# Order of the products in a projection, and the loading of the first panel, in a two-layer decoder trunk

## The chip, the cores and the metric

The kernel runs on one core of a Trainium2 chip. The metric is device time in microseconds (us) for one execution, as the median of several. Profiles come from a separate profiled execution, whose own time is given beside its span (from its first to its last instruction).

## The reference, cut to what matters

A trunk of two layers over 256 tokens of width 2048, with 256 memory tokens:

```python
mem_n = rmsnorm(mem, norm_mem)
for i in range(2):
    if i == 1:
        fk, fv, fc = fox_shared_kv(x, fox_kv_norm, fox_w_kv, fox_b_f)
    mk, mv = memory_kv(mem_n, mem_w_kv[i])
    h = rmsnorm(x, norm_mix[i])
    # layer 0: gated linear attention, layer 1: forgetting attention, both with 4 memory heads
    x = x + (gla_mixer if i == 0 else fox_mixer)(h, ..., mk, mv, ...)
    h = rmsnorm(x, norm_ffn[i])
    x = x + conv_ffn(h, ffn_w_up[i], ffn_conv_w[i], ffn_conv_b[i], ffn_w_down[i])
return rmsnorm(x, norm_final)
```

Nearly all of the arithmetic is projections: an activation of 256 tokens times a weight matrix of 2048 (or 5632) rows. All inputs and weights are 32-bit floats.

## The kernel before, in words

**Products in parts.** TensorE takes the weights and activations in a 32-bit format of its own (`F32R`) that keeps fewer bits than a float. So each float is split into a high part (a copy rounded to `F32R`) and a low part (the float minus its high part). A product is then three products: high times high, high times low, low times high. Activations lie as `[128, 2, 256]` tiles (`bufA`, `bufB`), high part and low part side by side, so one 512-wide matmul multiplies a weight's high part by both parts of an activation ("wide" or "high" product), and one 256-wide matmul multiplies a weight's low part by the activation's high part ("narrow" or "low" product).

**Units.** Weights are packed in HBM (`wp`) in units of 128 partitions x up to 1024 columns (512 KB), in the order of their use. `split_unit` (L204) and `load_unit` (L187) handle one unit: SyncE (SP) issues a DMA into `raw` (4 buffers, L198), ScalarE (ACT) casts it into `whi` (3 buffers, L201), VectorE (DVE) subtracts to give `wlo` (3 buffers, L210). They are put 300 places ahead in the priorities (`AHEAD`) from which the framework's scheduler writes each engine's queue; each engine then works its queue in order.

**Two kinds of panel.** `proj_fm` (L213) makes 256 output features by 256 tokens from four units of four 128-row chunks each: weights stationary, activations moving, two PSUM accumulators (`c` = 0, 1). For a unit it runs 8 wide products (L233) and 8 narrow ones (L231); the last unit runs its narrow ones first. Since the last unit of a panel ends with wide ones and the next panel begins with wide ones, a panel is, on TensorE, 16 wide (8 of them the last panel's), 8 narrow, 8 wide, 8 narrow, 8 wide, 16 narrow. `proj_tm` (L246) has the tokens stationary and up to 512 weight columns moving; it isn't changed but for the number of `wlo` buffers.

**What follows a panel.** An `evac` function takes the accumulator apart: `whole` (ACT L241, DVE L243), then, for an up-projection (`ffn`, 88 of the panels), a scaling (L860), the causal convolution (ACT L864, DVE L865, L866), the gate (L869, L870) and the split of the result (L306, L307). These share ACT's and DVE's queues with the casts and subtractions of the next units.

**The start.** `WARM` = 12 matmuls on a cleared tile (L178) come first. The first panel, `("mk", 0, 0)`, multiplies the memory. `take_mem` (L454) loads the memory in four groups of four chunks (`memt`; the gains of its norm lie ahead of the first group) and splits each chunk (`split`, L302: ACT L309 scales to the high part, DVE L310 computes the low part), beside the loads of the four units of weights, which are cast and subtracted in two pieces each. The first group's first half is issued on ACT's DMA queue, everything else on SP's. After the panel the squares of the memory are summed for its norm (L492 to L501).

**The end.** The last projection's `last` (L931) handles two blocks `b` of 128 tokens: it adds the accumulator to the residual `x[3]`, squares it, multiplies it by the final gain into `y` (L942), gets the root of the mean (L944 to L953), multiplies the four 512-wide parts by it (L957, L959) and stores each (L960), part 1 through ACT's queue and the others through SP's.

**Others that the change touches.** `att` (L529), two `[128, 384]` tiles cleared by GpSimd (POOL, L534), holds the attention of a linear-attention head. `mk[0]` holds the memory keys of layer 0; `mem_parts` (L412) splits it into parts and nothing reads it afterwards.

Of the kernel before, what the change touches and what calls it, by code (L numbers as in the profile page):

```python
# [12 lines left out]
F32 = mybir.dt.float32  # L13
# [28 lines left out]
WARM = 12  # L42
# [96 lines left out]
def _trunk(ctx: ExitStack, tc: tile.TileContext, xt, xtok, memt, wp, wgu, gns, gfin, cnv, par, msk, out):  # L139
# [30 lines left out]
    mk = [const.tile([P, MEM_H, T], F32, name=f"mk{l}") for l in range(2)]  # L170
# [16 lines left out]
    def load_unit(unit, pieces=1, before=None, pool=wpool, whole=False):  # L187
        off, kcs, n = unit
        w = len(kcs) * n
        raw = wpool.tile([P, NUNIT], F32, name="raw", tag="raw", bufs=4)  # L190
        hi = pool.tile([P, NUNIT], F32R, name="whi", tag="whi", bufs=3)
        src = wp[off : off + P * w].rearrange("(p n) -> p n", p=P)
        for i in range(pieces):
            if before is not None:
                before(i)
            s = slice(i * w // pieces, (i + 1) * w // pieces)
            if not whole:
                loads.append(nc.sync.dma_start(raw[:, s], src[:, s]))  # L198
            elif i == 0:
                loads.append(nc.sync.dma_start(raw[:, :w], src))  # L200
            casts.append(S.activation(hi[:, s], raw[:, s], AF.Copy))  # L201
        return raw, hi, w

    def split_unit(unit, pieces=1, before=None, pool=wpool, whole=False):  # L204
        with tc.high_priority(offset=AHEAD):
            raw, hi, w = load_unit(unit, pieces, before, pool, whole)
            lo = pool.tile([P, NUNIT], F32R, name="wlo", tag="wlo", bufs=3)
            for i in range(pieces):
                s = slice(i * w // pieces, (i + 1) * w // pieces)
                V.tensor_tensor(lo[:, s], raw[:, s], hi[:, s].bitcast(F32), ALU.subtract)  # L210
        return hi, lo

    def proj_fm(key, src, evac, before=None):  # L213
# [6 lines left out]
        for n, unit in enumerate(units):  # L220
            if before is None:
                hi, lo = split_unit(unit)
            else:
                hi, lo = split_unit(unit, 2, lambda half: before(n, half), whole=n > 0)
            steps = [(c, j, src[kc - base]) for j, kc in enumerate(unit[1]) for c in range(2)]
            final = n == len(units) - 1
            for part in ((1, 0) if final else (0, 1)):
                for c, j, both in steps:
                    s = slice(j * 256 + c * P, j * 256 + (c + 1) * P)
                    if part:  # L230
                        TE.matmul(acc[c][:, :T], lo[:, s], both[:, 0, :], start=False, stop=False)  # L231
                    else:
                        TE.matmul(acc[c], hi[:, s], both, start=n == 0 and j == 0,  # L233
                                  stop=final and j == len(unit[1]) - 1)
# [67 lines left out]
    def split(dst, i, src, g=None):  # L302

        hi, lo = dst[i][:, 0, :], dst[i][:, 1, :]
        if g is None:
            S.activation(hi, src, AF.Copy)  # L306
            V.tensor_tensor(lo, src, hi.bitcast(F32), ALU.subtract)  # L307
        else:
            S.activation(hi, src, AF.Copy, scale=g)  # L309
            V.scalar_tensor_tensor(lo, src, g, hi.bitcast(F32), ALU.mult, ALU.subtract)  # L310

# [138 lines left out]
    with tc.tile_pool(name="load", bufs=1) as lp:  # L450
        mraw = [lp.tile([P, KC + 4 * T], F32, name=f"mt{i}") for i in range(4)]
        mt = [t[:, KC:].rearrange("p (c t) -> p c t", t=T) for t in mraw]

        def take_mem(g, half):  # L454

# [577 lines left out]
```

## Time and profile before

| | |
|---|---|
| median of 3 runs | 2286.44 us (2286.3 to 2286.55) |
| the profiled execution | 2286.35 us |
| its span | 2284.6 us |
| TensorE matmul, busy | 2273.0 us, 12420 matmuls |
| VectorE, busy | 1613.1 us |
| ScalarE, busy | 1245.6 us |
| GpSimd, busy | 3.2 us, 20 instructions |
| read from HBM | 425.87 MB |

How to read it: PE is TensorE's matmuls and PEld its weight loads, DVE is VectorE, ACT ScalarE, POOL GpSimd, SP SyncE; a `q` behind the name is the engine's sequencer, which waits and issues DMAs. L210 is line 210 of the kernel before. In a group, `out<-in` are the tiles, then the count, busy us and mean ns of one, and after a second bar the idle time of the engine ahead of the group with what ended it. Matmuls overlap and their ends are modelled, so the time of a matmul is read from one start to the next. In the timeline a row is start us, length us, engine, line and what it does, merged over neighbours of one kind.

### The profile page before, as it was taken

Reading aid. Unit: us, or ns where it says so; the run is one execution under the profiler, and the core shown is the slowest. Engines: PE = TensorE matmul, PEld = TensorE weight load, DVE = VectorE, ACT = ScalarE, POOL = GpSimd, SP = SyncE. Lnnn points to the kernel's source line nnn. Section 1 sums busy time; section 2 is a strip of 40 time slices with the busy share of each in tenths; the row PEclk is TensorE's granted clock in tenths of the full one; section 3 lists DMA queues with packets and bytes.
Section 4 is the critical chain, followed back from the end, with each engine's and each line's share of the span. In section 5 each row is a group of like instructions: output and inputs, shape, how many; then the busy total and the mean of one; then the engine's idle time right before and its main releaser. Section 6 shows DMA issues by size and latency. Waiting matters only on the chain.

```text
span 2284.6 us, 33316 instructions
## 1 busy us (share of the span) xinstructions
PE 2273.0 (99%) x12420; PEld 1983.1 (87%) x12420; DVE 1613.1 (71%) x2691; ACT 1245.6 (55%) x1981; POOL 3.2 (0%) x20
## 2 busy tenths in 40 slices
PE   9999999999999999999999999999999999999998
PEld 8889988888888888888888998888888888888886
DVE  8679997577765777567766568657776577756775
ACT  7556555555543555445565555556554455534554
POOL 0000000000000000000000000000000000000000
PEclk9999999999999999999999999999999999999999
DMA  9555555555555555555555664556555655555564
GB/s 330 190 166 162 164 164 189 184 187 192 185 194 194 189 189 187 195 190 190 190 184 186 181 196 158 178 186 186 192 186 192 193 188 191 189 195 188 189 191 155
DMA packets 124746, 430.16 MB, mean 188 GB/s; under 512 B 14108, under 2 KB 18600, under 8 KB 124456
## 3 DMA queue, kind: packets, MB, share of 16 engines
q1 hardware_dynamic: 124152, 427.24, 57.7%
q8 instruction: 97, 1.59, 0.3%
q10 hardware_dynamic: 432, 0.79, 0.1%
q14 instruction: 65, 0.53, 0.1%
HBM read 425.87 MB, written 2.11 MB: 187 GB/s over the span
## 4 chain that ended last, share of the span: by engine, by line
PE 99%; DVE 1%; DMA 0%; issue 0%; ACT 0%; DVEq 0%
PE acc L233 39%; PE acc L271 36%; PE acc L231 20%; PE ps_s L890 0%; PE ps_s L645 0%; PE ps_t L402 0%; PE ps_s L423 0%; PE ps_o L423 0%; DVE A L310 0%; PE ps_s L802 0%; PE ps_o L818 0%; PE ps_o L689 0%; DVE wlo L210 0%; DMA raw<-wp 0%; PE ps_s L801 0%; PE ps_o L690 0%
## 5 line engine op out<-in xcount | busy, mean ns | idle before, releaser
L210 DVE TENSOR_TENSOR wlo<-raw,whi 128x1024 fp32r<-128x1024 f32 (+4 forms) x812 | 971.3, 1197 | 446.5 <-ACT whi L201 431.4
L201 ACT ACTIVATE whi<-raw 128x1024 fp32r<-128x1024 f32 (+4 forms) x812 | 842.1, 1038 | 634.7 <-PE acc L271 327.0
L233 PE MATMUL acc<-B,whi 128*128 128x512 f32 x2112 | 524.0, 392 | 0.0
L233 PEld LDWEIGHTS acc<-B,whi 128*128 128x128 f32 x2112 | 382.1, 189 | 69.9
L271 PE MATMUL acc<-whi,mix 128*128 128x512 f32 x1280 | 320.3, 390 | 0.0
L233 PE MATMUL acc<-mix,whi 128*128 128x512 f32 x1248 | 315.7, 393 | 0.0
L231 PEld LDWEIGHTS acc<-B,wlo 128*128 128x128 f32 x2112 | 280.7, 191 | 15.8 <-DVE wlo L210 0.2
L231 PE MATMUL acc<-B,wlo 128*128 128x256 f32 x2112 | 288.2, 283 | 0.0
L271 PEld LDWEIGHTS acc<-whi,mix 128*128 128x128 f32 x1280 | 239.7, 188 | 49.8
L233 PEld LDWEIGHTS acc<-mix,whi 128*128 128x128 f32 x1248 | 227.1, 188 | 42.0
L241 ACT ACTIVATE part<-acc 128x256 f32<-128x256 f32 x240 | 90.2, 376 | 243.8 <-PE acc L233 243.6
L271 PE MATMUL acc<-whi,B 128*128 128x512 f32 (+3 forms) x960 | 217.9, 362 | 0.0
L243 DVE TENSOR_TENSOR wholes<-acc,part 128x256 f32<-128x256 f32 x240 | 100.8, 420 | 133.5 <-ACT part L241 133.5
L271 PEld LDWEIGHTS acc<-whi,B 128*128 128x128 f32 x960 | 174.5, 188 | 17.7
L231 PEld LDWEIGHTS acc<-mix,wlo 128*128 128x128 f32 x1248 | 171.4, 190 | 12.2
L231 PE MATMUL acc<-mix,wlo 128*128 128x256 f32 x1248 | 177.0, 283 | 0.0
L271 PE MATMUL acc<-wlo,mix 128*128 128x512 f32 x640 | 173.9, 390 | 0.0
L271 PEld LDWEIGHTS acc<-wlo,mix 128*128 128x128 f32 x640 | 119.9, 188 | 24.8
L233 PE MATMUL acc<-A,whi 128*128 128x512 f32 x544 | 136.5, 393 | 0.3 <-DVE A L310 0.2
L864 ACT ACTIVATE cv<-u,cw 128x256 f32<-128x256 f32 x176 | 105.0, 598 | 46.5 <-DVE u L860 46.5
L271 PE MATMUL acc<-wlo,B 128*128 128x512 f32 (+3 forms) x480 | 120.8, 363 | 0.9 <-DVE wlo L210 0.9
L233 PEld LDWEIGHTS acc<-A,whi 128*128 128x128 f32 x544 | 97.8, 189 | 18.7 <-DVE A L310 0.7
(225 smaller groups left out, 1602.0 us busy)
## 6 DMA issues: line engine op xcount, KB each, us to landing
raw<-wp SPq DMA_DIRECT2D x743, 512.0 KB, 3.5
raw<-wp SPq DMA_DIRECT2D x32, 384.0 KB, 3.3
raw<-wp SPq DMA_DIRECT2D x24, 388.0 KB, 3.6
raw<-wp SPq DMA_DIRECT2D x8, 400.0 KB, 3.2
xf<-xt SPq DMA_DIRECT2D x16, 128.0 KB, 4.8
x<-xtok SPq DMA_DIRECT2D x4, 512.0 KB, 8.4
mt<-memt SPq DMA_DIRECT2D x3, 512.0 KB, 6.5
cb<-cdram SPq DMA_DIRECT2D x12, 128.0 KB, 3.3
```

The lines of the kernel that those rows point to most:

```text
L201: casts.append(S.activation(hi[:, s], raw[:, s], AF.Copy))
L210: V.tensor_tensor(lo[:, s], raw[:, s], hi[:, s].bitcast(F32), ALU.subtract)
L231: TE.matmul(acc[c][:, :T], lo[:, s], both[:, 0, :], start=False, stop=False)
L233: TE.matmul(acc[c], hi[:, s], both, start=n == 0 and j == 0, stop=final and j == len(unit[1]) - 1)
L241: S.activation(t, a[:, T:], AF.Copy)
L243: V.tensor_tensor(r, a[:, :T], t, ALU.add)
L271: mm = TE.matmul(acc[b][:, :n], src[kc - base][:, part, xs], w, start=u == 0 and low == part == j == 0, stop=u == end and low == 1 and j = ...
L864: S.activation(r, u[:, 2:], AF.Identity, bias=w[3], scale=w[2])
```

## The change

The core of the diff (lines that only rename or pass an argument are left out):

```diff
-WARM = 12
+WARM = 9
...
+    def split_unit(unit, pool=wpool):
...
+            raw = wpool.tile([P, NUNIT], F32, name="raw", tag="raw", bufs=4)
+            hi = pool.tile([P, NUNIT], F32R, name="whi", tag="whi", bufs=3)
+            lo = pool.tile([P, NUNIT], F32R, name="wlo", tag="wlo", bufs=4)
...
+        if before is None:
+            turns = [(0, 0), (1, 0), (0, 1), (1, 1), (2, 1), (3, 1), (2, 0), (3, 0)]
+        else:
+            turns = [(0, 0), (0, 1), (1, 0), (1, 1), (2, 0), (2, 1), (3, 1), (3, 0)]
+        ready = {}
+        chunks = [(u, low, j) for u, low in turns for j in range(4)]
+        if before is not None:
+            chunks[:8] = sorted(chunks[:8], key=lambda t: t[2])
+        for u, low, j in chunks:
+            if u not in ready:
+                ready[u] = split_unit(units[u]) if before is None else before(u, units[u])
+                if u == 1 and between is not None:
+                    between()
+            w, both = ready[u][low], src[units[u][1][j] - base]
+            for c in range(2):
+                s = slice(j * 256 + c * P, j * 256 + (c + 1) * P)
+                if low:
+                    TE.matmul(acc[c][:, :T], w[:, s], both[:, 0, :], start=False, stop=False)
+                else:
+                    TE.matmul(acc[c], w[:, s], both, start=u == j == 0, stop=(u, j) == (3, 3))
...
     def split(dst, i, src, g=None, alone=False):
...
-            S.activation(hi, src, AF.Copy, scale=g)
+            done = V.tensor_scalar(hi, src, g, None, ALU.mult) if alone else S.activation(hi, src, AF.Copy, scale=g)
             V.scalar_tensor_tensor(lo, src, g, hi.bitcast(F32), ALU.mult, ALU.subtract)
...
+        lead = [lp.tile([P, KC + 4 * 512], F32, name=f"ld{g}") for g in range(2)]
+        pair = [t[:, KC:].rearrange("p (c k t) -> p c k t", k=2, t=T) for t in lead]
+        mt = [t[:, :, 1, :] for t in pair]
+        mt += [lp.tile([P, 4, T], F32, name=f"mt{g}") for g in range(2, 4)]
+
+        def first_unit(g, unit):
+            off, kcs, n = unit
+            hi = wpool.tile([P, NUNIT], F32R, name="whi", tag="whi", bufs=3)
+            lo = wpool.tile([P, NUNIT], F32R, name="wlo", tag="wlo", bufs=4)
             if g == 0:
+                S.preload_act_table_set("natural_log_exp_and_others")
+            with tc.high_priority(offset=AHEAD):
+                if g < 2:
+                    step = 1 if g == 0 else 2
+                    for c in range(0, 4, step):
+                        at = slice(KC + c * 512 if c else 0, KC + (c + step) * 512)
+                        if g:
+                            at = slice(KC + c * 512, KC + (c + step) * 512)
+                        loads.append(nc.sync.dma_start(lead[g][:, at], memt[g, :, at]))
+                    w = pair[g][:, :, 0, :]
+                else:
+                    step = 2
+                    raw = wpool.tile([P, NUNIT], F32, name="raw", tag="raw", bufs=4)
+                    loads.append(nc.sync.dma_start(raw, wp[off : off + P * NUNIT].rearrange("(p n) -> p n", p=P)))
+                    loads.append(nc.sync.dma_start(mt[g].rearrange("p c t -> p (c t)"), memt[g, :, KC : KC + 4 * T]))
+                    if g == 2:
                         nc.sync.dma_start(gains, gns)
+                    w = raw.rearrange("p (c t) -> p c t", t=T)
+                for c in range(0, 4, step):
+
+                    for i in range(c, c + step):
+                        k = 4 * g + i
+                        done = split(bufA, k, mt[g][:, i, :], lead[0][:, k : k + 1], i % 2 == 1)
+                        if i % 2 == 0:
+                            casts.append(done)
+                    cs = slice(c, c + step)
+                    h3, l3 = (t.rearrange("p (c t) -> p c t", t=T)[:, cs, :] for t in (hi, lo))
+                    casts.append(S.activation(h3, w[:, cs, :], AF.Copy))
+                    nc.gpsimd.tensor_tensor(l3, w[:, cs, :], h3.bitcast(F32), ALU.subtract)
+            return hi, lo
...
+        proj_fm(("mk", 0, 0), bufA, first_out, before=first_unit)
+        proj_fm(("mk", 0, 1), bufA, mk_out(0, 1), between=squares)
...
-            for t in (*att, *ks):
+            for t in ks:
                 nc.gpsimd.memset(t, 0.0)
...
             kv = mem_parts(0, "A")
+
+            lent = const.tile([P, MEM_H, T], F32, name="att", tag="mk0").rearrange("p f t -> p (f t)")
+            nc.gpsimd.memset(lent, 0.0)
+            att = [lent[:, i * 3 * P : (i + 1) * 3 * P] for i in range(2)]
...
-            V.tensor_tensor(y[:, b, :], x[3][:, b, :], gf[:, 3 * 512 :], ALU.mult)
...
-            for g in range(4):
-                t = y[:, b, :] if g == 3 else x[g][:, b, :]
-                if g == 1:
+            for f, lo, hi in ((0, 0, T), (1, 0, 512), (0, T, 512), (2, 0, 512), (3, 0, 512)):
+                t = x[f][:, b, lo:hi]
+                if f == 1:
                     S.activation(t, t, AF.Copy, scale=r)
+                elif f < 3:
+                    V.tensor_scalar(t, t, r, None, ALU.mult)
                 else:
-                    V.tensor_scalar(t, t, r, None, ALU.mult)
-                (nc.scalar if g == 1 else nc.sync).dma_start(out[b, :, g * 512 : (g + 1) * 512], t)
+                    V.scalar_tensor_tensor(t, t, r, gf[:, 3 * 512 :], ALU.mult, ALU.mult)
+                (nc.scalar if f == 1 else nc.sync).dma_start(out[b, :, f * 512 + lo : f * 512 + hi], t)
```

What it does, part by part:

- **Order of the products.** In every panel of `proj_fm` but the first, the units' products run as high 0, high 1, low 0, low 1, low 2, low 3, high 2, high 3. Each unit is loaded, cast and subtracted whole; `wlo` has four buffers.
- **The first panel.** The first two groups of memory and the first two units of weights lie interleaved in one array, 256 columns of weights beside 256 columns of memory. Group 0 is loaded in four pieces, group 1 in two, groups 2 and 3 as weights and memory apart, all on SP's queue. The first unit's products alternate by chunk, two wide and two narrow. Every second memory chunk's high part is computed on DVE, the others on ACT; the weights are cast on ACT and their low parts subtracted on POOL, in pieces of 256 columns (unit 0) or 512 (the others).
- **The squares** of the memory come inside the second panel, behind its second unit's load.
- **The warm-up** has nine matmuls.
- **`att`** lies in the place of `mk[0]`, and is cleared once `mem_parts` is through.
- **The end.** `y` is gone: part 3 is multiplied by the root and the gain in one instruction. Part 0 is scaled and stored in two halves, around part 1.

More of the change, by code (lines that the diff above doesn't have):

```diff
@@ L219, in proj_fm @@
         base = min(min(u[1]) for u in units)
[L220 to L234, printed above, removed]
+        if before is None:
[18 more added lines that the diff above has]
+                    TE.matmul(acc[c], w[:, s], both, start=u == j == 0, stop=(u, j) == (3, 3))
         for c in range(2):
```

81 lines of the change are left out of this document (26 added, 55 removed).

## The prediction

> **What bounds the kernel now.** I read first the totals and the chain that ended last on the page, then the groups of the three projection lines, then the timeline of one up-projection, of the first 20 us and of the last 10 us.
>
> ```profile
> PE 2273.0 (99%) x12420; PEld 1983.1 (87%) x12420; DVE 1613.1 (71%) x2691; ACT 1245.6 (55%) x1981; POOL 3.2 (0%) x20
> ...
> PE 99%; DVE 1%; DMA 0%; issue 0%; ACT 0%; DVEq 0%
> ...
> L233 PE MATMUL acc<-B,whi 128*128 128x512 f32 x2112 | 524.0, 392 | 0.0
> L233 PE MATMUL acc<-mix,whi 128*128 128x512 f32 x1248 | 315.7, 393 | 0.0
> L233 PE MATMUL acc<-A,whi 128*128 128x512 f32 x544 | 136.5, 393 | 0.3 <-DVE A L310 0.2
> ```
>
> PE is busy for 99% of the span and is 99% of the chain. L233, the 512-wide high product of `proj_fm`, has 2112 + 1248 + 544 = 3904 matmuls. A panel has 32 of them, so there are 122 such panels, each with 32 narrow low products (L231) beside them. PE waits for nobody there: idle before it is 0.0 or 0.3 us. What can still go is what PE spends inside its own stream, what it waits for in the first panel, and the end after its last product.
>
> One panel, on PE alone (start, length, line, tiles, count; the next row's start tells when a run is over, the printed lengths overlap):
>
> ```profile
> 599.78 1.48 PE L231 MATMUL acc<-B,wlo 128*128 128x256 f32 x11
> 601.10 3.82 PE L233 MATMUL acc<-B,whi 128*128 128x512 f32 x16
> 604.76 1.12 PE L231 MATMUL acc<-B,wlo 128*128 128x256 f32 x8
> 605.71 2.00 PE L233 MATMUL acc<-B,whi 128*128 128x512 f32 x8
> 607.55 1.11 PE L231 MATMUL acc<-B,wlo 128*128 128x256 f32 x8
> 608.50 2.00 PE L233 MATMUL acc<-B,whi 128*128 128x512 f32 x8
> 610.34 2.08 PE L231 MATMUL acc<-B,wlo 128*128 128x256 f32 x16
> ```
>
> And rows of the chain in order of time (start, length, count):
>
> ```profile
> 844.45 3.65 PE acc L233 x16
> 877.91 3.65 PE acc L233 x16
> 913.21 87.04 PE acc L271 x384
> ```
>
> A 512-wide product in a long run takes 87.04 / 384 = 0.2267 us. A 256-wide one inside a run takes (601.10 - 599.78) / 11 = 0.120 us. A panel therefore needs 32 x 0.2267 + 32 x 0.120 = 11.093 us. Its period is (877.91 - 844.45) / 3 = 11.153 us. The missing 0.060 us lies in the three times per panel that PE goes from wide to narrow and back: 0.020 us each. The rows bear it out: 16 wide ones take 3.66 us, 8 take 1.84, which is 0.02 over 8 x 0.2267.
>
> **The change, part by part.**
>
> *Longer runs.* The new `turns` put a panel as high 0, 1, low 0 to 3, high 2, 3: one there-and-back instead of three. 121 panels (the first has its own order) x 2 x 0.020 us = **-4.84 us**. The instructions are the same; nothing is added to PE. From below the gain could be zero, if the 0.020 us isn't paid at the switch; it can't be more, as no other excess is left in the period.
>
> What the order asks of the others: low 3 is wanted 6.5 us into its panel (16 wide, 24 narrow) instead of 8.4, and high 1 at 1.8 instead of 2.8. `whi` keeps three buffers, so the cast of unit 3 can begin when high 0 is done, at 1.8, and the cast of the next unit 1 when high 2 is done, at 9.3, for use at 12.9. The fourth `wlo` buffer lets low 0 to 3 lie ready together.
>
> ```profile
> L210 DVE TENSOR_TENSOR wlo<-raw,whi 128x1024 fp32r<-128x1024 f32 (+4 forms) x812 | 971.3, 1197 | 446.5 <-ACT whi L201 431.4
> L201 ACT ACTIVATE whi<-raw 128x1024 fp32r<-128x1024 f32 (+4 forms) x812 | 842.1, 1038 | 634.7 <-PE acc L271 327.0
> ...
> L866 DVE SCALAR_TENSOR_TENSOR cv<-u,cw,cv 128x256 f32<-128x256 f32 x176 | 83.9, 478 | 0.0
> ```
>
> Cast (1.04) and subtraction (1.20) end at 1.8 + 2.2 + 0.1 = 4.1; 2.4 us are left until 6.5. I cost it at nothing. The cover is these 2.4 us; ahead of a subtraction in DVE's queue stand pieces of the previous panel's evacuation, up to 0.48 us each like L866.
>
> *The first panel.*
>
> ```profile
> 1.45 4.80 PE L178 MATMUL ps_o<-B 128*128 128x512 f32 x12 [1.45 <-DVE B L175]
> 4.67 0.63 ACT L201 ACTIVATE whi<-raw 128x512 fp32r<-128x512 f32 x1 [2.21 <-DMA raw<-wp]
> 5.94 1.67 DVE L310 SCALAR_TENSOR_TENSOR A<-mt,A 128x256 fp32r<-128x256 f32 x4
> 6.48 2.19 PE L233 MATMUL acc<-A,whi 128*128 128x512 f32 x8 [0.22 <-DVE A L310]
> 12.76 1.70 ACT L309 ACTIVATE A<-mt,mt 128x256 fp32r<-128x256 f32 x4
> 14.36 1.14 ACT L201 ACTIVATE whi<-raw 128x512 fp32r<-128x512 f32 x2
> 17.21 3.82 PE L233 MATMUL acc<-A,whi 128*128 128x512 f32 x16
> ...
> 2.00:14.00 12.00, 11.67 (x50) 9.13 (x49) 8.67 (x19) 9.78 (x23) 0.00 (x0) 1.00 1.02 384
> ```
>
> The panel's last 8 wide products are the first half of the 16 at 17.21: it ends at 17.21 + 1.84 = 19.05. Its own work is 11.1 us and it begins at 6.48, so 1.5 us are waits. The last row is a stretch of time (busy time of PE, PEld, DVE, ACT, POOL, then clock, DMA share, GB/s): from 2 us on DMA is full. Eight times 512 KB of first weights and memory and the gains, 4.24 MB, pass at 384 GB/s until 13.0; with the notice the last is usable near 13.6, an estimate that holds before and after. One array with 1 KB pieces beside each other brings the first chunk to about 3.9 (half of what shared the queue until 4.67), and the first product to about 5.1, where nine warm-up products end too (1.45 + 9 x 0.40). These 1.4 us are hidden: the last data sets the end. SP issues 11 transfers, where it had 10 and ACT one. At 0.42 us an issue (the L960 row at the end) that is under 5 us for 11 us of transfers, and what is queued behind them (`mask`, the next weights) waits for DMA anyway.
>
> So what counts is the work behind the last data. The weights' low halves go from DVE to POOL, and every second memory chunk's high half from ACT to DVE. The nearest rows:
>
> ```profile
> L310 DVE SCALAR_TENSOR_TENSOR A<-mt,mt,A 128x256 fp32r<-128x256 f32 x12 | 5.0, 480 | 0.0
> L400 DVE TENSOR_SCALAR p<-p,rc 128x256 f32<-128x256 f32 x16 | 5.1, 349 | 0.1
> L210 DVE TENSOR_TENSOR wlo<-raw,whi 128x512 fp32r<-128x512 f32 x8 | 5.2, 687 | 3.9 <-ACT whi L201 3.9
> ...
> L534 POOL MEMSET ks<- 128x512 f32 x2 | 1.0, 528 | 48.8 <-PE acc L271 48.8
> L283 POOL MEMSET narrow<- 128x256 f32 x2 | 0.6, 314 | 758.3 <-DMA raw<-wp 758.3
> ```
>
> No row shows POOL subtracting. From below it costs a memset, 0.53 us for 512 columns; a memset only writes. From above, two inputs and one output at the memset's pace of (528 - 314) / 256 = 0.84 ns a column: 0.1 + 3 x 0.43 = 1.39 us (0.74 for 256). I take the upper one, because of the two reads. The Trainium skill, GPSIMD Engine Reference, section "Elementwise — side-by-side cycle accounting", puts a two-input operation at about 2.6 cycles of 1.2 GHz an element. That is an estimate of 1.1 us and would end the panel some 0.7 us earlier; no trace here shows it yet.
>
> 512 KB take 1.3 us, so the third group's memory is there 2.6 us before the fourth's, at 11.0. ACT's high half (0.40, the pace of the four at 12.76) and cast (0.52, of the two at 14.36) follow, so POOL works from 11.95 to 14.73 on two pieces, and on the fourth group's two until 17.51. Then four narrow products (0.48) and eight wide (1.84): the panel ends at 19.83, **+0.8 us**. From below: if ACT casts a group's weights, which land 1.3 us ahead of its memory, first, POOL is ready by 16.8 and DVE's four L310 and two scalings of the last group (about 2.5 us after 14.1) decide: end near 18.5, -0.5. From above: the rival of the turns.
>
> The squares move into the second panel (four on ACT); they are wanted only by the norm behind the third. `att` in `mk0`'s place is cleared on POOL long before the heads. Both cost nothing.
>
> *The end.*
>
> ```profile
> 2276.94 0.69 DVE L942 TENSOR_TENSOR y<-x,gf 128x512 f32<-128x512 f32 x1
> 2277.33 0.19 ACT L941 ACTIVATION_READ_ACCUMULATOR sq<-x 128x1 f32 x1
> 2277.55 0.15 DVE L944 SCALAR_TENSOR_TENSOR fv<-sums,fp 128x1 f32<-128x1 f32 x1
> 2277.80 0.16 DVE L944 SCALAR_TENSOR_TENSOR fv<-sums,fv 128x1 f32<-128x1 f32 x1
> 2279.58 0.81 SPq L960 DMA_DIRECT2D out<-x  x2
> 2280.48 0.42 SPq L960 DMA_DIRECT2D out<-y  x1
> ...
> 2280.25:2283.25 3.00, 0.00 (x0) 0.00 (x0) 0.09 (x1) 0.00 (x0) 0.00 (x0) 0.50 0.91 350
> ```
>
> Without `y` the first L944 needn't wait for L942, and the second follows ACT's sum at 2277.52: 0.25 us sooner. Half a tile first lets the first store go 0.2 us sooner still. The last row moves 1.05 MB, all four stores, at 91%: DMA-bound, so the end moves with the first store, -0.45; if the extra issue on SP (0.45) decides, 0. I take **-0.4**.
>
> **Sum.** The profiled execution took 2286.35 us (span 2284.6 and 1.75 around it), 0.09 under the median 2286.44. -4.84 + 0.8 - 0.4 = -4.4: 2281.9, against the median **2282.0 us**.
>
> **The rivals.**
>
> *Weights are cast first and POOL keeps up (0.20).* First panel -0.5 instead of +0.8: 2280.7, down to 2280.2 at the memset's price. For it: ACT at 4.67 took the weights that had landed before a memory chunk. Against it: the casts stand behind the high halves in the program, as at 12.76 and 14.36.
>
> *DVE and POOL take turns (0.30).*
>
> ```profile
> 38.52 1.22 DVE L210 TENSOR_TENSOR wlo<-raw,whi 128x1024 fp32r<-128x1024 f32 x1
> 38.71 0.78 POOL L534 MEMSET att<- 128x384 f32 x2 [37.74 <-DVE B L310]
> ```
>
> Both read two operands from SBUF all through this panel. If only one can read at a time, their work adds up: DVE 16 x 0.40 (the pace of the four at 5.94) + 8 x 0.27 (L400 less the same 0.08) = 8.5 us, POOL 4 x 0.74 + 6 x 1.39 = 11.3, from 4.4 on until 24.2, and 2.3 of products: 26.5, or +7.4: 2288.6. With POOL at DVE's own 0.42 and 0.69 it is 5.8, 18.7, 21.0: 2283.2. The middle is 2286. For it: nothing in this trace, where POOL reads nothing; the clearing at 38.71 left the DVE subtraction beside it at its usual 1.22, but it only writes. The Trainium skill, SBUF — State Buffer, section "Who interferes with whom", states just this: a DVE instruction with two SBUF inputs, or a scaling in its fast mode, and a GpSimd instruction that reads SBUF exclude each other for the whole instruction. No run here shows it yet; by that rule this rival is what comes.
>
> *PE starves for low halves (0.08).* In each of the 88 up-projections low 3 must be there 1.9 us sooner. It decides from the point where over 2.4 us of evacuation, five of its ten DVE pieces, stand ahead of that subtraction. Each 0.1 us by which it is late costs 8.8 us: at 0.15 it is +13, or 2295, slower. Against it: ten pieces among four subtractions, so two or three to each if they spread.
>
> *The switch isn't what costs (0.06).* Then -4.84 falls away: 2286.8.
>
> **Chances.** Forecast 0.36 (2281.3 to 2283). A measurement of this kernel tells about 0.2% from no change, here 4.57 us: faster means under 2281.87. Faster: 0.20 and 0.13 of the forecast, 0.33. Slower (over 2291.0): 0.08 and 0.02 of the turns, 0.10. Within: 0.57. The range from 2280.2 (weights first) to 2289.0 (turns at the dear price) leaves out starving and little else.
>
> **What would show it.** In the changed profile, a panel's period in the chain should be 11.11 us, with runs of 32. L210 should never be a releaser of PE by more than a few us in all. In the first panel, POOL's subtraction lasts 1.39 us for 512 columns, or far more with gaps if turns are taken, and L310 with it; the second panel's products start near 20, 18.5 or over 22 us. The last store should be issued at about the same distance from the end of PE, and DMA should finish 0.4 us sooner. The forecast is wrong if PE's idle time past 25 us grows, or if the period stays 11.15.

## The result, and the profile after

The changed kernel takes **2291.73 us** (median of 12 runs, 2290.04 to 2293.00), the kernel before 2286.45: a ratio of 1.0021, 95% interval 1.0013 to 1.0029. It is 5.3 us slower, where 4.4 us less were forecast and 2289.0 was the top of the range. The profiled execution of the changed kernel took 2290.13 us, span 2288.1; it is one of its quickest, which comes up again below.

The page after: totals, the chain that ended last, and the high products of the panels that multiply `A` (L233 is now L226, L231 is L224, L210 is L197, L309 and L310 are L301 and L302):

```profile
PE 2270.3 (99%) x12417; PEld 1984.1 (87%) x12417; DVE 1608.0 (70%) x2691; ACT 1247.5 (55%) x1975; POOL 14.5 (1%) x29
...
PE 97%; DVE 2%; DMA 0%; issue 0%; ACT 0%; SPq 0%; DVEq 0%
...
L226 PE MATMUL acc<-A,whi 128*128 128x512 f32 x544 | 135.9, 392 | 5.5 <-DVE A L302 4.9
```

PE still fills its span, but it is 97% of the chain instead of 99%, and 4.9 us of idle time are now put down to L302, the memory's low halves.

**The steady part.** Rows of the chain after, in order of time, in the first feed-forward layer:

```profile
1102.38 7.28 PE acc L226 x32
1109.66 2.87 PE acc L224 x24
1112.53 1.84 PE acc L226 x8
1114.37 0.95 PE acc L224 x8
1115.32 5.47 PE acc L226 x24
1120.79 3.83 PE acc L224 x32
1124.62 7.28 PE acc L226 x32
```

Runs of 32 are there, and 7.28 + 3.83 = 11.11 us is the panel that was forecast. But only every second panel is like that; the one between goes 24, 8, 8, 24, with two there-and-backs. The scheduler that writes PE's queue put high 2 ahead of low 3 there. Two panels take 1124.62 - 1102.38 = 22.24 us, not 22.22.

**The gated layer.** PE and DVE near the end of the first mixer, from the timeline after:

```profile
295.91 2.37 PE L224 MATMUL acc<-B,wlo 128*128 128x256 f32 x16
296.92 0.42 DVE L319 TENSOR_TENSOR ssq<-sq 128x256 f32<-128x256 f32 x1
297.26 0.42 DVE L235 TENSOR_TENSOR wholes<-acc,part 128x256 f32<-128x256 f32 x1
297.59 0.41 DVE L626 TENSOR_SCALAR gq<-gq,get 128x64 f32<-128x64 f32 x2
297.91 0.56 DVE L643 TENSOR_TENSOR gde<-bc 128x384 f32<-128x384 f32 x1
298.38 1.22 DVE L197 TENSOR_TENSOR wlo<-raw,whi 128x1024 fp32r<-128x1024 f32 x1
299.66 1.21 PE L224 MATMUL acc<-B,wlo 128*128 128x256 f32 x8 [1.38 <-DVE wlo L197]
```

PE has done two units' low products and wants the third's at 298.1. Five pieces of the layer's own work stand ahead of that subtraction in DVE's queue, and PE waits 1.38 us (from start to start it is 1.54 us more than the usual 0.120). There are two more such waits, 1.28 us at 283 (for `att`, DVE L701) and 0.20 at 296.7: 3.02 us, where the kernel before has one of 1.03 us (start to start, beyond the usual 0.173) at 312:

```profile
313.30 0.97 PE L271 MATMUL acc<-wlo,B 128*128 128x384 f32 x4 [0.86 <-DVE wlo L210]
```

**The first panel.** The timeline after, PE, DVE, ACT and POOL:

```profile
11.53 2.78 DVE L302 SCALAR_TENSOR_TENSOR A<-ld,ld,A 128x256 fp32r<-128x256 f32 x2
12.58 5.44 POOL L483 TENSOR_TENSOR wlo<-raw,whi 128x512 fp32r<-128x512 f32 x4
14.45 1.64 PE L226 MATMUL acc<-A,whi 128*128 128x512 f32 x4 [2.94 <-DVE A L302]
15.47 0.91 ACT L301 ACTIVATE A<-mt,ld 128x256 fp32r<-128x256 f32 x2 [0.16 <-DMA mt<-memt]
16.80 2.69 DVE L302 SCALAR_TENSOR_TENSOR A<-mt,ld,A 128x256 fp32r<-128x256 f32 x4
18.75 2.09 PE L226 MATMUL acc<-A,whi 128*128 128x512 f32 x8 [0.95 <-DVE A L302]
22.59 1.78 PE L226 MATMUL acc<-A,whi 128*128 128x512 f32 x7
```

Two L302 last 2.78 us beside POOL; four took 1.67 in the kernel before. The last eight wide products begin at 22.59, so the panel ends at 22.59 + 8 x 0.2267 = 24.40: 5.35 us later than the 19.05 of before. The groups of this stretch after:

```profile
L302 DVE SCALAR_TENSOR_TENSOR A<-mt,ld,A 128x256 fp32r<-128x256 f32 x8 | 4.3, 602 | 0.0
L302 DVE SCALAR_TENSOR_TENSOR A<-ld,ld,A 128x256 fp32r<-128x256 f32 x4 | 3.7, 954 | 0.1
L301 DVE TENSOR_SCALAR A<-mt,ld 128x256 fp32r<-128x256 f32 x4 | 3.3, 855 | 0.0
L483 POOL TENSOR_TENSOR wlo<-raw,whi 128x512 fp32r<-128x512 f32 x4 | 5.4, 1387 | 0.0
```

**The clock.** Stretches after (busy time of PE, PEld, DVE, ACT, POOL, then the granted clock, DMA share, GB/s):

```profile
13.00:15.00 2.00, 0.55 (x2) 0.48 (x3) 2.00 (x2) 1.45 (x4) 2.00 (x2) 0.98 1.03 406
15.00:17.00 2.00, 2.00 (x9) 1.77 (x8) 2.00 (x3) 1.42 (x4) 2.00 (x3) 0.50 0.97 364
17.00:19.00 2.00, 1.05 (x5) 0.75 (x5) 2.00 (x3) 0.86 (x1) 1.02 (x1) 0.66 0.72 269
```

After PE's idle stretch the clock is at half from about 14.9 to 18.3 us. In the kernel before its record shows full speed from 5.3 us to the end of PE's work.

**The end.**

```profile
2279.24 0.63 PE L263 MATMUL acc<-wlo,B 128*128 128x512 f32 x2
...
2282.94 1.81 SPq L979 DMA_DIRECT2D out<-x  x4
```

From the last pair of products to the first store of the last block it is 3.70 us. In the kernel before the pair began at 2275.49 and the store was issued at 2279.58: 4.09.

```profile
2275.49 0.63 PE L271 MATMUL acc<-wlo,B 128*128 128x512 f32 x2
```

The span ends 8.85 us after the pair instead of 9.07: 0.22 less.

**The sum**, against the profiled executions: +5.35 first panel, -3.84 there-and-backs (366 before, 176 after by the records, 190 x 0.0202), +1.99 waits in the gated layer (3.02 less 1.03), -0.22 end: +3.3. Measured is 2290.13 - 2286.35 = +3.8. Of the missing half microsecond 0.25 lies outside the spans, which differ by 3.53; the rest has no name here. Products that both traces hold confirm the stages: the changed kernel is 5.34 us behind after the first projections (30 us), 6.63 after the gated layer, 5.32 after the first feed-forward layer, 4.98 after the second mixer and 3.75 at PE's end. The median lies another 1.6 above the profiled execution.

### The profile page after: what moved, and what is told of

It reads as the page before. It is cut to its first block, busy times and chain, and to the rows that moved or that the text cites. A ratio compares the mean times of both kernels' runs of the same rounds, so it can differ in the third digit from the quotient of the medians.

```text
span 2288.1 us, 33322 instructions
## 1 busy us (share of the span) xinstructions
PE 2270.3 (99%) x12417; PEld 1984.1 (87%) x12417; DVE 1608.0 (70%) x2691; ACT 1247.5 (55%) x1975; POOL 14.5 (1%) x29
## 4 chain that ended last, share of the span: by engine, by line
PE 97%; DVE 2%; DMA 0%; issue 0%; ACT 0%; SPq 0%; DVEq 0%
PE acc L226 38%; PE acc L263 36%; PE acc L224 20%; PE ps_s L909 0%; DVE wlo L197 0%; PE ps_t L395 0%; PE ps_s L664 0%; DMA ld<-memt 0%; PE ps_o L416 0%; PE ps_s L416 0%; DVE A L302 0%; PE ps_s L821 0%; PE ps_o L837 0%; DVE att L701 0%; DVE A L301 0%; PE ps_o L708 0%
## 5 line engine op out<-in xcount | busy, mean ns | idle before, releaser
L197 DVE TENSOR_TENSOR wlo<-raw,whi 128x1024 fp32r<-128x1024 f32 (+2 forms) x804 | 965.7, 1202 | 579.5 <-ACT whi L196 577.2
L196 ACT ACTIVATE whi<-raw 128x1024 fp32r<-128x1024 f32 (+2 forms) x804 | 836.6, 1041 | 749.8 <-PE acc L263 342.4
L226 PE MATMUL acc<-B,whi 128*128 128x512 f32 x2112 | 503.4, 391 | 0.0
L226 PEld LDWEIGHTS acc<-B,whi 128*128 128x128 f32 x2112 | 389.0, 188 | 75.9
L226 PE MATMUL acc<-mix,whi 128*128 128x512 f32 x1248 | 307.7, 391 | 0.0
L224 PEld LDWEIGHTS acc<-B,wlo 128*128 128x128 f32 x2112 | 267.8, 191 | 9.4 <-DVE wlo L197 1.8
L224 PE MATMUL acc<-B,wlo 128*128 128x256 f32 x2112 | 273.3, 283 | 1.4 <-DVE wlo L197 1.4
L226 PEld LDWEIGHTS acc<-mix,whi 128*128 128x128 f32 x1248 | 228.9, 188 | 44.1
L224 PE MATMUL acc<-mix,wlo 128*128 128x256 f32 x1248 | 163.1, 284 | 0.0
L224 PEld LDWEIGHTS acc<-mix,wlo 128*128 128x128 f32 x1248 | 158.3, 191 | 4.5
L226 PE MATMUL acc<-A,whi 128*128 128x512 f32 x544 | 135.9, 392 | 5.5 <-DVE A L302 4.9
L226 PEld LDWEIGHTS acc<-A,whi 128*128 128x128 f32 x544 | 101.2, 188 | 27.4 <-ACT A L301 3.4
L233 ACT ACTIVATE part<-acc 128x256 f32<-128x256 f32 x240 | 90.8, 379 | 61.5 <-PE acc L226 61.2
```

Of the source, the lines that this page charges most:

```text
L196: casts.append(S.activation(hi[:, :w], raw[:, :w], AF.Copy))
L197: V.tensor_tensor(lo[:, :w], raw[:, :w], hi[:, :w].bitcast(F32), ALU.subtract)
L224: TE.matmul(acc[c][:, :T], w[:, s], both[:, 0, :], start=False, stop=False)
L226: TE.matmul(acc[c], w[:, s], both, start=u == j == 0, stop=(u, j) == (3, 3))
L233: S.activation(t, a[:, T:], AF.Copy)
```

## The experiments

**1. The first panel's low halves on DVE again.** The changed kernel with one word edited:

```diff
-                    nc.gpsimd.tensor_tensor(l3, w[:, cs, :], h3.bitcast(F32), ALU.subtract)
+                    V.tensor_tensor(l3, w[:, cs, :], h3.bitcast(F32), ALU.subtract)
```

> The changed kernel with one word edited: the first panel's low halves are subtracted on VectorE (DVE) instead of GpSimd (POOL); start, queue, orders and end stay. Theory (DVE and POOL take turns: DVE's 256-column rows, 0.48 us in the kernel before, show 0.60 to 0.95 us beside POOL's 0.74 and 1.3 us): DVE's rows go back to about 0.48 us (L302) and well under 0.8 us (the plain scalings, L301), a 512-column subtraction takes 0.69 us as in the kernel before. DVE then has 16 x 0.48 + 8 x 0.3 + 4 x 0.35 + 6 x 0.69 = 15.6 us of work from 4.6 us on, so its last subtraction ends near 20 and the panel near 21.5 instead of 24.4: about 2.9 us faster than the changed kernel, 2288 to 2289.5. Rival 1 (the long DVE rows are DVE's own, from the new array's strides or from the type of the operation): L301 stays at 0.83 to 0.86 us, DVE is loaded with 5.5 us more, the panel ends near 28: 2295. Rival 2 (the late data alone set the panel's end, the last chunk landing at 15.45 us): no change within 0.5 us, 2291.7.

Measured: 2286.34 us (2285.81 to 2286.64), 5.4 less than the changed kernel and level with the kernel before (0.9999, 0.9990 to 1.0008). The groups of its first 25 us:

```profile
L302 DVE SCALAR_TENSOR_TENSOR A<-mt,ld,A 128x256 fp32r<-128x256 f32 x8 | 3.3, 482 | 0.0
L483 DVE TENSOR_TENSOR wlo<-raw,whi 128x512 fp32r<-128x512 f32 x4 | 2.6, 686 | 0.0
L301 DVE TENSOR_SCALAR A<-mt,ld 128x256 fp32r<-128x256 f32 x4 | 1.2, 349 | 0.0
```

Same tiles, same strides: L302 602 to 482 ns, L301 855 to 349. So the long rows came from POOL's work beside them, and with some 5.8 us more to do (4 x 0.42 + 6 x 0.69) DVE is done sooner. The panel ends near 20.8; of the 5.35 us that it had lost, 1.7 stay with the new start. The gain is larger than expected (3.6 in the spans, 5.4 in the medians): the clock stays at full speed here, and the runs lie within 0.9 us.

**2. The old start, all else as changed.** The kernel before's loads and first panel, with the new turns, four `wlo`, `att` in `mk0`'s place and the new end.

> The changed kernel with the kernel before's start (its loads, its first panel, its mask loads) put back: the new order of products, the fourth buffer of low halves, the lent array for att and the new end stay. Theory: the first panel alone loses 5.35 us (end of the panel's last product 24.40 against 19.05 us); the rest gains 1.6 (fewer changes of form 3.84, more waiting in the gated layer 2.2) and the end 0.2. So 2286.45 - 1.8 = 2284.6, range 2284 to 2285.5, and the spread between runs falls back to that of the kernel before (0.5 us). Rival (the order of products is worth nothing, and the start lost less than the traces show): 2286.2 to 2287.

Measured: 2284.72 us (2284.56 to 2284.87; 0.9992, 0.9983 to 1.0001), as the theory said (2284.6). The interval just reaches 1, but all 11 runs lie below every run of the kernel before. The start alone loses 7.0 us of median; the rest gains 1.8.

**3. The old turns, all else as changed.**

```diff
-            turns = [(0, 0), (1, 0), (0, 1), (1, 1), (2, 1), (3, 1), (2, 0), (3, 0)]
+            turns = [(0, 0), (0, 1), (1, 0), (1, 1), (2, 0), (2, 1), (3, 1), (3, 0)]
```

> The changed kernel with only the list of turns in proj_fm put back to the old order (high and low halves by turns, the last unit's low half first); the new start, four low buffers and the new end stay. Theory: the there-and-backs between the two forms go back from 176 to 366 in the trace, 190 x 0.0202 = 3.8 us more, and the extra waits in the gated layer's first panels (1.28, 0.2 and 1.54 us against one of 1.03) go, 2.0 to 2.2 us less: 2291.7 + 1.7 = 2293.4, range 2292.5 to 2294.5, with one wait near 312 us as in the kernel before. Rival 1 (the waits in the gated layer come from the lent array for att and not from the order): they stay, 2291.7 + 3.8 = 2295.5. Rival 2 (a change of form costs nothing): 2289.5, faster than the changed kernel.

Measured: 2290.59 us (2290.03 to 2292.47; 1.0020, 1.0011 to 1.0029). The expectation missed: I had 2293.4. In the trace the there-and-backs are back and none of the three waits in the gated layer is left; the wait of 1.03 us at 312 is gone too, which I hadn't counted. There are 194 more there-and-backs than in the changed kernel, 3.9 us; 3.9 more and 3.0 less leave 0.9, and the spans differ by 0.3 (2288.4 against 2288.1). So rival 1 falls (the lent array is still there, the waits aren't), and the new turns as built were worth next to nothing. The medians can't be set against each other as they stand: in both kernels the runs fall into two groups (below), and more of this kernel's lie in the lower one.

**4. Runs of 32 in every panel.** The old start and new end, with three casts ahead of the first low half:

```diff
-            turns = [(0, 0), (1, 0), (0, 1), (1, 1), (2, 1), (3, 1), (2, 0), (3, 0)]
+            turns = [(0, 0), (1, 0), (2, 0), (0, 1), (1, 1), (2, 1), (3, 1), (3, 0)]
```

> As the kernel with the old start put back (new end, four low buffers), with the list of turns written so that three high halves are cast ahead of the first low half: high 0, 1, 2, low 0, 1, 2, 3, high 3. In the program this leaves 128 there-and-backs between the forms, against 372 in the kernel before and 177 in the changed one: nearly every panel runs its 32 wide and 32 narrow products together. Theory (each there-and-back costs 0.0202 us): (372 - 128) x 0.0202 = 4.9 us less than the kernel before, 0.2 less at the end: 2281.3 if the waits in the gated layer are those of the kernel before, 2283.5 if they are those of the changed one (2.2 us more). Rival 1 (the switch isn't what costs): 2286.2. Rival 2 (the low halves come too late when three casts go first): idle time of the matmul engine released by the low subtraction in each panel, over 2290.

Measured: 2285.36 us (2283.97 to 2285.73; 0.9993, 0.9984 to 1.0002): 1.1 less than the kernel before, not 2.9 to 5.1. The feed-forward layers do gain (PE gains 1.7 us on the kernel before in each, by products that both traces hold), but the gated layer loses 3.0. The timeline there, and a stretch right behind it:

```profile
317.10 0.97 PE L277 MATMUL acc<-wlo,B 128*128 128x384 f32 x4 [2.27 <-DVE wlo L210]
```

```profile
318.50:321.50 3.00, 3.00 (x11) 3.00 (x10) 2.94 (x8) 1.17 (x2) 0.00 (x0) 0.50 0.88 275
```

One wait of 2.27 us for a low half, and then 3 us at half clock, in which ten products of 384 columns take 0.32 instead of 0.173 us: 1.5 us more. Here a long wait is paid nearly twice. The runs fall into two groups, 2283.97 to 2284.41 and 2285.36 to 2285.73, and the profiled execution is the slowest of the upper one; that the lower group is the one without this drop is argued from the distance of 1.3 us, as only one run has a trace.

**5. Runs of 32 in the feed-forward layers alone.** As the run before, but

```diff
+        if key[0] == "up":
+            turns = [(0, 0), (1, 0), (2, 0), (0, 1), (1, 1), (2, 1), (3, 1), (3, 0)]
+        else:
+            turns = [(0, 0), (0, 1), (1, 0), (1, 1), (2, 0), (2, 1), (3, 1), (3, 0)]
```

> As the kernel with the old start and the three high halves first, but that list of turns is used only in the 88 up panels of the two feed-forward layers, where the vector engine has little besides the subtractions; all other panels keep the old order. Old start, four low buffers, new end. Theory (a there-and-back costs 0.0202 us everywhere, and what took the gain back is that in the gated layer the low halves are wanted early while VectorE is full of the layer's own work): 88 x 2 x 0.0202 = 3.55 us less than the kernel before, the wait of 1.03 us at 312 gone as in the run with the old order (four low buffers), 0.2 less at the end: 2286.45 - 4.8 = 2281.7, range 2281.2 to 2282.8. Rival (the loss is in the feed-forward layers or anywhere): 2285 or more, as with the new order in all panels.

Measured: **2281.27 us** (2281.10 to 2281.46; 0.9977, 0.9969 to 0.9986), 5.2 less than the kernel before and 10.5 less than the changed one. Its chain:

```profile
1095.82 7.28 PE acc L240 x32
1103.10 3.83 PE acc L238 x32
1106.93 7.28 PE acc L240 x32
1114.21 3.83 PE acc L238 x32
1118.05 7.28 PE acc L240 x32
```

(1118.05 - 1095.82) / 2 = 11.115 us a panel, every panel, and no wait of PE over 0.3 us anywhere past the first panel. By products that both traces hold, PE gains 1.73 us on the kernel before in the first feed-forward layer and 1.68 in the second, 3.41 where 3.55 were expected, nothing in the second mixer, and 1.55 in the gated layer, of which the wait of 1.03 us explains two thirds. By this the price of a there-and-back and the place of the loss are both shown.

**6. The probe: POOL beside DVE.** The kernel before, with work on POOL that nothing reads (`probe` is the layer's number, for every other unit of the up panels):

```diff
+                if probe:
+                    nc.gpsimd.tensor_copy(junk, hi[:, :512].bitcast(F32))
+                else:
+                    nc.gpsimd.tensor_tensor(junk, raw[:, :512], hi[:, :512].bitcast(F32), ALU.subtract)
```

> The kernel before, with work added on GpSimd that nothing reads: beside the subtraction of every other unit in the up panels a POOL instruction of 512 columns into one unused tile, released by the same cast as VectorE's subtraction. In the first feed-forward layer it has two inputs (a subtraction), in the second one input (a copy). Theory (DVE and POOL take turns at two-input work): in the first layer the DVE subtractions that have one beside them go from 1.22 us to 1.9 to 2.5 us, the POOL ones take 1.3 us or more; the panels still fit (DVE busy about 8 of 11.15 us, 2 x 1.0 more), so the time is 2286 to 2290. For the copies nothing here gives a number: if it is the two inputs that matter, DVE stays at 1.22 us in the second layer. Rival (the long rows of the changed kernel's first panel had another cause): 1.22 us in both layers, POOL 1.3 us, 2286.5.

Measured, one run: 2286.54 us. The timeline, DVE and POOL:

```profile
803.04 1.22 DVE L210 TENSOR_TENSOR wlo<-raw,whi 128x1024 fp32r<-128x1024 f32 x1
803.14 2.27 POOL L216 TENSOR_TENSOR junk<-raw,whi 128x512 f32<-128x512 f32 x1 [4.04 <-ACT whi L201]
804.18 0.42 DVE L249 TENSOR_TENSOR wholes<-acc,part 128x256 f32<-128x256 f32 x1
804.52 1.18 DVE L871 SCALAR_TENSOR_TENSOR cv<-u,cw,cv 128x256 f32<-128x256 f32 x1
...
818.92 1.35 POOL L216 TENSOR_TENSOR junk<-raw,whi 128x512 f32<-128x512 f32 x1 [2.34 <-ACT whi L201]
819.06 2.30 DVE L210 TENSOR_TENSOR wlo<-raw,whi 128x1024 fp32r<-128x1024 f32 x1
```

The time of the run says nothing, as both answers allow it; the rows do. Whoever starts first keeps its time, and the other waits until it is through. At 803 DVE's subtraction is 0.1 us ahead and takes its 1.22; POOL's takes 2.27, which is the 1.12 left of DVE's and 1.15 of its own. Then POOL holds DVE's L871 (0.48 alone) until 805.4: 1.18. At 818.9 POOL comes ahead of L210: it takes 1.35, as 0.21 of an earlier DVE piece were left, and L210 takes 2.30. My expectation had the right rule and the wrong victim: DVE mostly started first, so its L210 barely changed and the pieces behind it did. L249 ran untouched at 0.42 while POOL was at work; it reads `acc` from PSUM and only one operand from SBUF. The copies of layer 1 take 1.58 us on the mean and wait behind DVE in the same way (one took 1.60 where 1.13 of DVE's were left, so about 0.5 of its own), but hold DVE up less. The Trainium skill, SBUF — State Buffer, section "Who interferes with whom", says that the first to issue has the shared port pair for its whole instruction and the other blocks, and that a DVE instruction with at most one SBUF input doesn't contend unless it runs in one of its fast two-port modes; the rows agree on both. The plain scaling isn't spared: L301, which reads 256 columns and a scalar column from SBUF, took 855 ns beside POOL and 349 without it. Its pace is that of a fast mode: in the kernel before a scaling takes 349 ns for 256 columns (L400) and about 480 for 512 (L959), 0.51 ns a column, where the two-input subtraction needs 1.05 (687 ns for 512, 1224 for 1024). The Trainium skill, in the same section, counts scalings in such a mode among the instructions that need the pair; the trace agrees.

**7. POOL alone, in the old start.** The kernel before, with only its first panel's eight subtractions on POOL:

```diff
-                V.tensor_tensor(lo[:, s], raw[:, s], hi[:, s].bitcast(F32), ALU.subtract)
+                (V if before is None else nc.gpsimd).tensor_tensor(lo[:, s], raw[:, s], hi[:, s].bitcast(F32), ALU.subtract)
```

> The kernel before with only the first panel's eight low halves of 512 columns subtracted on POOL instead of VectorE; its loads, order and everything else stay. Theory (DVE and POOL take turns, one whole instruction each): 8 x 1.2 us of POOL and 16 x 0.42 us of DVE then stand one behind the other from 5 us on, 16.3 us, the last low half is there near 21, and 8 narrow and 8 wide products follow (0.96 + 1.84): the panel ends near 23.5 to 24 instead of 19.05 and the time is 2290 to 2291.5. Rival (side by side): the last cast ends near 15.3, two POOL subtractions and the products follow, the panel ends near 20.5: 2287.2 to 2288.

Measured: 2290.58 us (2290.41 to 2292.15; 1.0020, 1.0011 to 1.0028), +4.1. The groups of its first 25 us:

```profile
L210 POOL TENSOR_TENSOR wlo<-raw,whi 128x512 fp32r<-128x512 f32 x8 | 11.2, 1423 | 6.2 <-ACT whi L201 6.2
L310 DVE SCALAR_TENSOR_TENSOR A<-mt,mt,A 128x256 fp32r<-128x256 f32 x12 | 11.0, 990 | 0.0
```

L310 doubles from 480 to 990 ns. With the old loads and the old order the move to POOL by itself costs 4.1 us (4.07 in the spans), where the whole new start loses 5.35 in its trace.

**8 and 9. Dummy products against the drop of the clock.** The changed kernel with products into a bank that nothing reads. First 14 and 6 of them, hung on the chunk that PE was waiting for:

> The changed kernel with 20 dummy products of 512 columns in the first panel's idle time (14 behind the second unit's low products, 6 behind the third's; their sums go to a bank that nothing reads). Everything else stays, the low halves on POOL too. Theory (the idle stretch from 11.3 to 14.45 us let the granted clock fall to half from 14.9 to 18.3 us, and how long it stays down differs between runs, which is the 3 us of spread): the clock is at full speed through the panel, the runs lie within 0.8 us of each other, and the median falls to 2289.3 to 2290.5 (14 x 0.227 = 3.2 us fill a gap of 3.3). Rival 1 (the spread comes from the engines' turns or from the transfers): the spread stays at 2 us or more and the median at 2291.7. Rival 2 (the dummies stand ahead of real products): slower, 2292.5.

Measured: 2294.10 us, the median of five runs (2292.45 to 2295.06; 1.0035, 1.0021 to 1.0049). Rival 2: they ran after the gap, ahead of real products (16.46 to 19.6 us in its timeline). So it doesn't say what the drop costs. Then 13 and 6, hung on data that is there when PE falls idle:

```diff
+            if before is not None and (u, low, j) in ((1, 0, 1), (1, 1, 3)):
+                for i in range(13 if j == 1 else 6):
+                    TE.matmul(warm, w[:, s], both, start=True, stop=True)
```

> The changed kernel with 19 dummy products in the first panel again, but placed where the matmul engine idles: 13 behind the second group's first wide products (9 of them come ahead of the chunk before, where there is also idle time) and 6 behind its low ones. In the run before this the dummies hung on the chunk that the engine was waiting for, so they ran after the gap. The runs of the changed kernel fall into two groups, 2290.0 to 2290.5 and 2291.6 to 2293.0 us, the second with a lower mean clock (0.997 or 0.998). Theory (the second group is a longer or a second drop of the granted clock to half after idle time): the second group goes, all runs lie in 2289.5 to 2290.8, median near 2290.1; the panel itself ends no earlier, since the wide products at 18.75 us wait for VectorE. Rival (the drop doesn't come from idle time, or costs nothing): still two groups, median 2291.7.

Measured: 2290.45 us, all runs in 2290.18 to 2290.95 (1.0017, 1.0008 to 1.0026). The upper group is gone, and with it 1.3 us of median. The stretches:

```profile
13.00:15.00 2.00, 1.25 (x6) 0.70 (x4) 2.00 (x2) 1.44 (x3) 2.00 (x2) 1.00 1.03 414
15.00:17.00 2.00, 1.29 (x7) 1.14 (x8) 2.00 (x3) 0.94 (x3) 2.00 (x3) 1.00 1.01 405
17.00:19.00 2.00, 2.00 (x13) 1.61 (x12) 2.00 (x4) 1.03 (x1) 1.01 (x1) 1.00 0.65 257
```

The clock holds. It does not make the profiled panel shorter: in the changed kernel the wide products at 18.75 us wait for DVE, and here they start at 19.05, straight behind the last dummies. The dearer runs of the changed kernel have a lower mean clock, 0.997 or 0.998; that their drop was longer is argued from this, as only one of its runs has a trace.

**10. All scalings on ACT.** Experiment 1 with DVE also freed of the memory's high halves (the last argument of `split` left out):

> The changed kernel with the first panel's low halves on VectorE (as in the first experiment) and in addition all 16 scalings of the memory's high halves on ScalarE (ACT), none on VectorE. Theory (in the first experiment VectorE's chain, without a gap from 9.8 to 20.8 us, sets the panel's end): it loses 8 scalings of 0.26 to 0.35 us, 2.1 to 2.8 us; ACT gets 8 of 0.41 to 0.51 us and had about 3.5 us idle there; the panel ends near 19.3 instead of 20.8: 2284.3 to 2285.6. Rival 1 (ACT's order becomes the bound): the panel ends at 20.8 or later, 2286.3 or more. Rival 2 (the transfers set it, last landing 15.45 us): the panel ends within 0.4 us of 20.8.

Measured: 2285.67 us (2285.30 to 2286.61; 0.9997, 0.9989 to 1.0006), 0.67 less than experiment 1, half of what was expected. DVE is done 1.1 us sooner, but the profiled execution, at 2286.53 us one of the two slowest, doesn't show the gain: PE waited 1.19 and 0.62 us near 9 and 10.5 us and then had half clock from 11.2 to 14.7, so its panel ends at 20.8 as well. It still isn't as good as the old start (experiment 2, by 0.95 us).

## Why the prediction was wrong, point by point

**What bounds the kernel.** Right for PE's own stream, the first panel and the end. The fourth place, the waits in the gated layer, was left out.

**The price of a there-and-back.** Right: 0.020 us was predicted; experiment 5 has 11.115 us a panel, and its two feed-forward layers gain 3.41 us where 88 x 2 x 0.0202 = 3.55 were expected from the turns. The rival that the switch isn't what costs is refuted.

**"121 panels x 2 x 0.020 us."** The count failed. I took the list of turns for the order on PE. The scheduler kept it in every second panel only, 190 there-and-backs went, not 242: -3.84, not -4.84. Why it breaks the list is argued, not shown: unit 3's cast waits for the `whi` buffer of unit 0, and in the scheduler's own estimate low 3 then comes after high 2. A list that puts three casts first was kept.

**"I cost it at nothing. The cover is these 2.4 us."** This is one of the steps that failed. The cover was worked out from the up panels, and there it holds: no wait in the feed-forward layers after. In the gated layer five pieces stand ahead of the subtraction, just the point from which the rival of starving was said to decide, but I had priced that rival for the 88 up panels only. It cost 3.02 us where 1.03 were, and ate half of the turns' gain.

**The first panel, "+0.8 us": the step that decides.** It measured +5.35. POOL's price was near (1.39 us taken; about 1.15 of its own in the probe, 1.31 to 1.42 with its waits), and in the first two groups the memory went ahead of the weights as assumed (in the others ACT cast the weights first). What failed was the layout of the sum: POOL's chain was laid beside DVE's as if each could run on its own. They took turns, instruction by instruction, so that the 11.3 us of POOL (4 x 0.783 + 2 x 1.314 + 4 x 1.387) stood in DVE's way, and PE waited for DVE's L302, not for POOL. Experiments 1, 6 and 7 show it from three sides. The rival of the turns had this with the panel's end from 21.0 to 26.5 (24.40 came), and I gave it 0.30 against 0.36. Nothing in the trace of before could decide between them, as I said; the rule of the Trainium skill, SBUF — State Buffer, section "Who interferes with whom", spoke for the turns, and I let the missing row count against it. By that rule the rival should have had the greater chance.

**"The last is usable near 13.6, an estimate that holds before and after."** Wrong: ACT's row at 15.47 waits for the last memory until then. From 2 to 6 and from 6 to 10 us the transfers move 273 and 373 GB/s, where the kernel before has 322 and 414. The late data isn't the bound in the changed kernel, where the third group's L302 at 18.7 us is; in experiment 1, with DVE's chain for this panel gapless from 9.8 to 19.5, its share isn't separated. The new start without POOL still ends 1.6 us behind the old one (2286.34 against 2284.72), and how that splits between late data and DVE's added scalings stays open, but for the 0.67 us of experiment 10.

**The end, "-0.4".** The first store came 0.39 us sooner, as worked out, and the span ends 0.22 sooner: -0.22. That the fifth issue, at 0.45 us each, took the rest back is argued, not shown.

**Not in the prediction at all:** the clock. I had no idle time of PE in the forecast, so no drop; PE's 2.94 us of waiting brought one, and with dummy products in the idle time the drop and 1.3 us of the median are gone (experiment 9).

**Added up.** -4.4 forecast, +4.55 for the first panel, +1.0 for the count, +1.99 for the waits and +0.18 for the end make +3.3; +3.8 was measured in the profiled execution, and the median lies 1.6 above that.

## What to carry to other kernels

Two engines that seem free side by side may have to take turns: before work is moved to GpSimd, ask which VectorE instructions with two SBUF operands (or fast scalings) run at that moment, and add the two up instead of laying them beside each other. A new order is worth what the queues of the *busiest* stage allow; here one list (experiment 4) gains 3.4 us in the feed-forward layers, where the other engines have room, and loses 3.0 in the gated layer, where they don't, so use it by stage. And read the order that the scheduler wrote, not the list in the program.

## What the runs showed of the hardware that was not expected

- A wait of PE of 2.3 to 2.9 us can be followed by 3.41 us at half clock, so that it is paid again with up to 1.5 us (experiment 4: ten 384-column products at 0.32 us). Whether it is depends on how the wait lies. In the clock record of the twelve traces all four drops in mid-kernel last 3.41 us, and every stretch at full clock is a whole multiple of that: 10.24 us ahead of the drop in the changed kernel, 6.83 in experiment 10, 314.03 in experiment 4. Cut into such windows, with the product times above (0.2267, 0.173 and 0.120 us), PE is idle for 3.01 us in the window ahead of the drop in the changed kernel, 3.09 in experiment 3, 2.32 in experiment 10 and 2.27 in experiment 4; no other window at full clock in any trace has more than 2.05. That one is in the run with the misplaced dummies, whose wait of 2.94 us fell into two windows (2.05 and 1.65 us idle) and brought no drop. In experiment 10 waits of 1.19 and 0.62 us and smaller gaps fell into one. The Trainium skill, TensorE: Matmul & The Clock Gate, section "Part 1: The HAM clock gate (the "warmup" mystery)", speaks of a free-running activity window of about 3.4 us; these records agree.
- POOL subtracts 512 columns with two inputs in about 1.15 us of its own (2.27 less the 1.12 that it waited); beside DVE both engines' rows grow (DVE 480 to 990 ns, POOL to 1423).
- A scaling of 512 columns takes DVE 480 ns, the subtraction 687, and yet the scaling is held up by POOL too (349 to 855 ns for 256 columns).
- A DVE instruction with one operand in PSUM keeps its 0.42 us beside POOL.
